# Letting two small stores wait for a row maximum instead of queueing behind the last load

## The chip, the cores and the metric

The kernel runs on one core of a Trainium2 chip. The metric is the device time of one execution in microseconds (us); the medians below are over several executions. SyncE is the engine that issues the transfers here, VectorE and GpSimd compute. A semaphore is a hardware counter that engines raise and wait for.

## The reference

```python
def setup_inputs():
    return {"x": np.random.randn(8192, 8192).astype(np.float32)}

def reference(x):
    return np.linalg.norm(x, ord=np.inf, axis=1)
```

The output is, for each of 8192 rows, the largest absolute value of 8192 float32 numbers: 268 MB are read, 32 KB written.

## The kernel before

SyncE issues all loads on one queue; VectorE takes a maximum over each loaded piece. The first 5888 rows come as 23 loads of 8 MB (two rows per partition). The last 2304 rows (18 per partition) come as 25 loads whose width shrinks to 1280 and 1152 columns, so that little is left to reduce when the last byte has landed (the last maximum reads 1156 columns: 1152 and four partial maxima of its row that lie behind them). Each load signals one of eight semaphores; a load counts as landed when its semaphore has got 16 increments, and the maximum waits for that.

```python
    def load(self, at, w, src):
        ...
        ins = self.nc.sync.dma_start(out=self.ring[:, at : at + w], in_=src)
        ins.then_inc(self.sems[i % SEMS], 16)
        ...
        if i >= SEMS:        # not before the load eight earlier is reduced
            self.tc.add_manual_dep(ins.ins, self.last[i - SEMS].name, ...)
```

The end of the program has three stores. Two of them (23 KB and 8 KB) are ready early; the third holds the last two of the 18 tail rows and needs the last maximum. GpSimd combines the partial maxima of rows that came in pieces, and SyncE waits for the last combination before the third store.

```python
    tc.declare_fence(done.ins, group="loads")
    nc.sync.dma_start(                                            # 128 x 46 floats, 23 KB
        out=out[:split].rearrange("(p q) -> p q", p=P), in_=res_big.rearrange("p t r -> p (t r)")
    )
    out_tail = out[split:].rearrange("(p r) -> p r", p=P)
    nc.sync.dma_start(out=out_tail[:, : ROWS - 2], in_=res_tail[:, : ROWS - 2])   # 8 KB

    seen = nc.sync.keepalive_nop(...)                             # waits for GpSimd
    ...
    last = nc.sync.dma_start(out=out_tail[:, ROWS - 2 :], in_=res_tail[:, ROWS - 2 :])  # 1 KB
```

## Time and profile before

| | before |
|---|---|
| time, median of 3 | 629.49 us |
| the profiled execution itself | 629.77 us, span 627.8 us |
| VectorE busy | 551.9 us (88%) |
| DMA | 428 GB/s over the span |

Read it from the end. Nearly all of the span is one long read, and the question is only what follows the last packet of it: when the last load counts as landed, when the last maximum starts, and when the last store lands. The lines for this are in the prediction.

### The profile page before, as it was taken

What the parts mean: (1) busy time and instruction counts of PE and PEld (TensorE: products, weight loads), DVE (VectorE), ACT (ScalarE), POOL (GpSimd) and SP (SyncE); (2) the same over time, 40 slices, a digit from 0 to 9 for tenths busy, and PEclk for the clock granted to TensorE, in tenths of its full rate; (3) what the DMA queues carried; (4) which work ended last, traced back from release to release, by engine and by line L of the source; (5) the groups of instructions that cost most, each with busy time, mean ns of one, the idle gap of its engine ahead of it and who ended that gap; (6) DMA issues with size and microseconds to landing.
All of it is one profiled execution on the core that took longest, in us unless ns stands there. A gap on an engine that the chain in (4) does not pass through costs nothing.

```text
span 627.8 us, 164 instructions
## 1 busy us (share of the span) xinstructions
DVE 551.9 (88%) x56; POOL 2.9 (0%) x13
## 2 busy tenths in 40 slices
DVE  0588988889988889888898888998889899999998
POOL 0000000000000000000000000000000000000000
DMA  9999999999999999999999999999999999999997
GB/s 401 413 455 409 459 405 463 405 463 401 468 401 468 401 468 401 468 401 468 401 468 401 468 401 468 401 468 401 468 390 435 452 419 438 426 422 431 427 422 284
DMA packets 7344, 268.47 MB, mean 428 GB/s; under 512 B 1200, under 2 KB 1200, under 8 KB 1968
## 3 DMA queue, kind: packets, MB, share of 16 engines
q1 hardware_dynamic: 7344, 268.47, 99.2%
HBM read 268.44 MB, written 0.03 MB: 428 GB/s over the span
## 4 chain that ended last, share of the span: by engine, by line
DMA 59%; DVE 40%; issue 0%; SPq 0%
DMA ring<-in_x_dram 59%; DVE res_big L106 22%; DVE parts L106 10%; DVE res_tail L106 8%; SPq L88 0%
## 5 line engine op out<-in xcount | busy, mean ns | idle before, releaser
L106 DVE TENSOR_REDUCE res_big<-ring 128x2 f32<-128x16384 f32 x23 | 396.1, 17220 | 69.3 <-DMA ring<-in_x_dram 69.3
L106 DVE TENSOR_REDUCE res_tail<-ring 128x1 f32<-128x8192 f32 (+1 forms) x10 | 79.0, 7945 | 2.6 <-DMA ring<-in_x_dram 2.6
L106 DVE TENSOR_REDUCE parts<-ring 128x1 f32<-128x3520 f32 (+17 forms) x19 | 69.8, 3738 | 1.7 <-DMA ring<-in_x_dram 1.7
L106 DVE TENSOR_REDUCE ring<-ring 128x1 f32<-128x1984 f32 (+3 forms) x4 | 7.7, 1982 | 0.0
L202 POOL TENSOR_SCALAR res_tail<-parts 128x1 f32<-128x1 f32 x8 | 2.3, 291 | 614.0 <-DVE parts L106 614.0
L202 POOL TENSOR_SCALAR parts<-parts 128x1 f32<-128x1 f32 x1 | 0.4, 357 | 7.0 <-DVE parts L106 7.0
L237 POOL MEMSET const-bfloat16-1.0<- 128x1 bf16 x1 | 0.1, 103 | 0.0
L237 POOL MEMSET const-uint8-127<- 128x1 uint8 x1 | 0.1, 102 | 0.0
L237 POOL MEMSET const-float32-0.0<- 128x1 f32 x1 | 0.1, 99 | 0.2 <-issue 0.2
L237 POOL MEMSET const-float32-1.0<- 128x1 f32 x1 | 0.1, 99 | 0.0
## 6 DMA issues: line engine op xcount, KB each, us to landing
ring<-in_x_dram SPq DMA_DIRECT2D x3, 4096.0 KB, 41.9
ring<-in_x_dram SPq DMA_DIRECT2D x1, 7488.0 KB, 31.1
ring<-in_x_dram SPq DMA_DIRECT2D x1, 6368.0 KB, 35.4
ring<-in_x_dram SPq DMA_DIRECT2D x1, 5920.0 KB, 40.8
ring<-in_x_dram SPq DMA_DIRECT2D x1, 4800.0 KB, 32.8
ring<-in_x_dram SPq DMA_DIRECT2D x1, 3488.0 KB, 40.4
ring<-in_x_dram SPq DMA_DIRECT2D x1, 3104.0 KB, 39.2
ring<-in_x_dram SPq DMA_DIRECT2D x1, 2944.0 KB, 40.8
```

What stands on the lines that cost most here:

```text
L106: ins = self.nc.vector.tensor_reduce(out=dst, in_=src, axis=mybir.AxisListType.X, op=mybir.AluOpType.max, apply_absolute_value=True,)
L202: combined = nc.gpsimd.tensor_scalar(out=to, in0=best, scalar1=two[0], scalar2=two[1] if len(two) == 2 else None, op0=mybir.AluOpType.max, ...
L237: nc = _bacc.Bacc("TRN2", target_bir_lowering=False, num_devices=1)
```

## The change

The intent is that the two early stores do not stand right behind the last load in the DMA rings, the queues from which the DMA engines take their work. They wait for the last maximum but one (the 1280-column piece), so that they run while VectorE is busy with the last one.

```diff
-    nc.sync.dma_start(
+
+    early = nc.sync.dma_start(
         out=out[:split].rearrange("(p q) -> p q", p=P), in_=res_big.rearrange("p t r -> p (t r)")
     )
     out_tail = out[split:].rearrange("(p r) -> p r", p=P)
-    nc.sync.dma_start(out=out_tail[:, : ROWS - 2], in_=res_tail[:, : ROWS - 2])
+    middle = nc.sync.dma_start(out=out_tail[:, : ROWS - 2], in_=res_tail[:, : ROWS - 2])
+    for store in (early, middle):
+        tc.add_manual_dep(
+            store.ins,
+            pieces.last[-2].name,
+            mybir.DependencyInfo(mybir.DependencyClass.Sync, mybir.DependencyReason.DATA),
+            reason="not beside the last load",
+        )
```

## The prediction

> **What bounds the kernel now.** I read the head of the page first, to see which resource is short over the whole span.
>
> ```profile
> span 627.8 us, 164 instructions
> DVE 551.9 (88%) x56; POOL 2.9 (0%) x13
> DMA  9999999999999999999999999999999999999997
> GB/s 401 413 455 409 459 405 463 405 463 401 468 401 468 401 468 401 468 401 468 401 468 401 468 401 468 401 468 401 468 390 435 452 419 438 426 422 431 427 422 284
> ```
>
> The DMA digits are 9 in every slice but the last. The kernel reads 268.4 MB at 428 GB/s, and 39 of 40 slices cannot change with a diff that touches two stores of 23 and 8 KB near the end. Only the last slice (7 and 284 GB/s) is open. So I asked for the last piece of the chain that ended last, and for the timeline there (columns: start in us, duration in us, engine, line, operation, tiles; in brackets the idle time before it and what ended that).
>
> ```profile
> 609.24 14.89 DMA ring<-in_x_dram
> 624.13 0.02 issue
> 624.15 1.36 DVE res_tail L106
> ```
>
> ```profile
> 622.22 1.48 DVE L106 TENSOR_REDUCE parts<-ring 128x1 f32<-128x1280 f32 x1
> 623.87 0.28 POOL L202 TENSOR_SCALAR res_tail<-parts 128x1 f32<-128x1 f32 x1 [8.68 <-DVE parts L106]
> 624.15 1.36 DVE L106 TENSOR_REDUCE res_tail<-ring 128x1 f32<-128x1156 f32 x1 [0.46 <-DMA ring<-in_x_dram]
> 625.54 0.33 SPq L222 DMA_DIRECT2D out_dram<-res_tail  x1
> ```
>
> The end is a chain: the last load lands at 624.13, the last maximum runs from 624.15 for 1.36 us, the last store is issued at 625.54, and 1.4 us after that it lands. VectorE was free from 622.22 + 1.48 = 623.70 and sat idle for 0.46 us until the load landed. That 0.46 us is the only slack that the change can reach. The DMA view of 609 to 628 us gives each issue's time to landing (count, KB, us):
>
> ```profile
> ring<-in_x_dram SPq DMA_DIRECT2D x1, 576.0 KB, 14.9
> out_dram<-res_big SPq DMA_DIRECT2D x1, 23.0 KB, 14.7
> out_dram<-res_tail SPq DMA_DIRECT2D x1, 8.0 KB, 14.4
> out_dram<-res_tail SPq DMA_DIRECT2D x1, 1.0 KB, 1.4
> ```
>
> The two early stores (23 and 8 KB) are issued at 609.61 and 610.09, right behind the last load (609.24), queue behind eight loads, and land at the same moment as the load whose landing ends the kernel. The last store alone needs 1.4 us.
>
> **Did the stores delay that load?** The answer is in the trace's DMA packets and semaphore increments, which no printed view lists; a load counts as landed at the last of 16 increments. From the first to the last of them the third last load takes 0.43 us (620.09 to 620.51) and the second last 0.44 us (621.67 to 622.11). The last load takes 1.04 us (623.09 to 624.13): nine increments come on time, within 0.31 us, and the other seven trail. Its data were not late. Its last data packet ends at 623.05; the second last load's ends at 621.63, and that load has landed 0.48 us later. The last load needs 1.08 us for the same step. In just that stretch run the stores' packets: 128 of 184 bytes starting from 622.54 to 623.14 and 128 of 64 bytes from 622.64 to 623.22, on engines that had finished their share of the load. Without them I expect the load to land at 623.05 + 0.48 = 623.53. A second way agrees: the second last load (5120 bytes per partition) landed 1.60 us after the one before it; 4608/5120 of that is 1.44, and 622.11 + 1.44 = 623.55.
>
> **What the Trainium skill says.** "DMA: Bandwidth & Descriptors", section "Queues, rings and completion order": on each DMA engine descriptors are taken in ring order, data descriptors carry no barrier, and the semaphore increment is a strongly ordered write that lands only after every earlier write of that engine. Stores queued behind a load can thus overlap its increments; the packets above show the overlap. The page does not say that a later store holds an earlier increment back, so that link is my inference from the 1.04 against 0.44 us. "Perfetto Trace Analysis", section "DMA Instruction — HWDGE (DVE, Sync)": the profiled issue ends when the sequencer is free, and data movement and completion come after it, with a delay that can be surprisingly long when the target is HBM. The trace agrees in kind: the last store's issue is 0.33 us of its 1.42 us to landing, its packets start 0.83 us after the issue began and the last landing comes 0.4 us after the last packet.
>
> **The change, part by part.** Removed: nothing; all three stores and their packets remain. Added: one wait on the DVE semaphore at the first store. The compiled order of instructions on every engine is the same in both kernels, and the second store follows the first in SyncE's order. The loads, the reductions and GpSimd's combinations are untouched. Moved, in steps:
>
> 1. The wait is for the maximum of the 1280-column piece, which ends at 623.70. In this trace SyncE starts about 0.02 us after the increment it waits for, itself some 0.01 us after the instruction's end. So the first store is issued at 623.73 instead of 609.61. It occupies the queue for 0.43 us, then 0.05 us pass (in before 609.61 to 610.09 is 0.48), so the second is issued at 624.21 and SyncE is free at 624.64.
> 2. The last load lands at about 623.54 instead of 624.13: 0.6 us earlier.
> 3. The last maximum cannot use all of it: VectorE is busy to 623.70. It starts at 623.72, after the 0.02 us seen between neighbours. Gain: 624.15 - 623.72 = 0.43 us. It ends at 623.72 + 1.36 = 625.08.
> 4. GpSimd's last combination (623.87 to 624.15) waits on the 1280-column maximum and does not move; it runs beside the last maximum, as earlier ones ran beside theirs without lengthening them (1156 columns with no GpSimd: 1357 ns; 3776 columns with it: 4078 ns; both are 1.04 ns a column plus about 0.15 us).
> 5. The last store needs that combination (624.15), the free queue (624.64) and the last maximum (625.08 + 0.02). The maximum is last by 0.4 us, so the store goes out at 625.10 instead of 625.54 and lands 1.42 us later, at 626.52 instead of 626.96.
> 6. The early stores, given the 1.42 us of the lone store plus 0.1 us for their longer issue, land at about 623.73 + 1.52 = 625.25 and 624.21 + 1.52 = 625.73, both 0.8 us before the last one. The kernel's closing waits then see the last store only.
>
> Sum: -0.43 us, and 629.49 - 0.43 = 629.06 us (span about 627.4).
>
> **The rivals.**
>
> - *The load's late landing is its own.* It is the last in the queue, and perhaps its increments trail because nothing follows it, not because stores do. For it: there is no second load in this trace that ends a queue. Against it: the very last store, with nothing behind it, gets its 16 increments within 0.19 us, and 9 of the load's 16 are on time. Then VectorE still starts at 624.15 and nothing is gained: 629.45 to 629.5.
> - *The stores become the new tail.* If the writes to HBM take over 0.8 us longer than my 1.52 us, the closing wait is for them, or the last store, whose 8-byte pieces lie in the same 72-byte rows as the second store's 64-byte pieces, is held behind them. For it: 256 small packets now enter within 2 us of the end. Against it: in before the same packets took 15 and 11 ns each, 16 of them per engine, or about 0.2 us, and the rings are otherwise empty now. It would eat 0 to 0.8 us: 629.1 to 629.9.
> - *SyncE becomes the bound.* Two issues of 0.48 us fit between 623.73 and 624.69 and the last store wants 625.10. If the issue were delayed by 0.4 us or more, it would push the store one for one. Against: the descriptor work of both was 0.43 us with eight loads in flight, and now the queues are empty. Worth at most a few tenths.
> - *Half the load's delay stays*, for example because it comes from closing traffic in general. VectorE idle would shrink from 0.46 to 0.1 or 0.2 us: about 629.2.
>
> None of these touches more than 2 us of 629: 2% is 12.6 us, and the whole section after the last load's landing is 3.7 us long.
>
> **Range and chances.** The runs of before agree within 0.01 us, so the spread is that of the mechanism. The gain is capped by VectorE at 0.44 us, hence little room below 629.05; I allow 0.15 us there for the closing part to be quicker with fewer things outstanding. Upward I go to no gain at all, 629.50. I give the full gain some 65%, a part of it 15%, none 12%, a loss of some tenths 8%. Within 2%: 99%.
>
> **What would show it.** Right: the last maximum follows its neighbour with no idle time and starts near 623.72; the early stores land in 1.4 to 1.7 us, not 14.7; the last load lands 14.3 us after its issue instead of 14.9, its 16 increments within about 0.45 us; the last store is issued near 625.10 and everything before 609 us is unchanged. Wrong: 0.46 us of idle time still stand before the last maximum (first rival); the early stores land after 626.5, or the last store takes clearly more than 1.42 us (second); the last store is issued well after the last maximum has ended (third). A change of 1 us or more would mean that something before 609 us moved, which this reading excludes.

## The result, and the profile after

The changed kernel took 629.38 us (median of 6, 629.35 to 629.59), the kernel before 629.49 us (median of 6, 629.43 to 629.65). The ratio is 0.9998, 95% interval 0.9986 to 1.0011. A ratio here is the mean time of one kernel's fast runs over that of the other's of the same rounds, so it is not quite the ratio of the medians. The interval includes 1, so these runs alone do not tell the gain from none. The 0.11 us between the medians is a quarter of the 0.43 us foreseen.

The head of the page of the changed kernel (without its GB/s row) is the same but for single tenths:

```profile
span 627.5 us, 164 instructions
DVE 551.8 (88%) x56; POOL 2.8 (0%) x13
DMA  9999999999999999999999999999999999999997
```

Its timeline from 622 us (start in us, duration in us, engine, line, operation, tiles):

```profile
622.47 1.48 DVE L106 TENSOR_REDUCE parts<-ring 128x1 f32<-128x1280 f32 x1
623.86 1.35 DVE L106 TENSOR_REDUCE res_tail<-ring 128x1 f32<-128x1156 f32 x1
623.98 0.35 SPq L213 DMA_DIRECT2D out_dram<-res_big  x1
624.13 0.28 POOL L202 TENSOR_SCALAR res_tail<-parts 128x1 f32<-128x1 f32 x1 [8.69 <-DVE parts L106]
624.37 0.43 SPq L217 DMA_DIRECT2D out_dram<-res_tail  x1
625.24 0.33 SPq L230 DMA_DIRECT2D out_dram<-res_tail  x1
```

There is no bracket with idle time at the last maximum any more. It starts 1.39 us after its neighbour (1.93 before), and the last store is issued 2.77 us after that neighbour's start (625.24 - 622.47; before 625.54 - 622.22 = 3.32). The DMA view from 609 us (KB, us from issue to landing):

```profile
ring<-in_x_dram SPq DMA_DIRECT2D x1, 576.0 KB, 14.3
out_dram<-res_big SPq DMA_DIRECT2D x1, 23.0 KB, 1.5
out_dram<-res_tail SPq DMA_DIRECT2D x1, 8.0 KB, 2.1
out_dram<-res_tail SPq DMA_DIRECT2D x1, 1.0 KB, 1.4
```

The last load lands 0.6 us sooner after its issue, exactly as intended, and its 16 increments spread over 0.57 us like those of the load before it (0.59 us), instead of 1.04 against 0.44.

So the profile shows a larger gain in the tail than the prediction, and the time a much smaller one. Between these two profiled executions the books balance: from the start of the 1280-column maximum to the landing of the last store, 4.75 us before and 4.17 us after, a gain of 0.58; but that maximum started 0.25 us later after the first load's issue (621.75 instead of 621.50), because already the first load landed 0.24 us later (21.98 instead of 21.74 us). The two profiled times differ by 629.77 - 629.44 = 0.33 us, and 0.58 - 0.25 is that. The 0.24 us arose before anything that the change touches. The open question is the 0.58: why do medians not show it?

### The profile page after: what moved, and what is told of

Same layout as the page of the kernel before. It is cut to its first block, busy times and chain, and to the rows that moved or that the text cites. A ratio compares the mean times of both kernels' runs of the same rounds, so it can differ in the third digit from the quotient of the medians.

```text
span 627.5 us, 164 instructions
## 1 busy us (share of the span) xinstructions
DVE 551.8 (88%) x56; POOL 2.8 (0%) x13
## 4 chain that ended last, share of the span: by engine, by line
DMA 57%; DVE 42%; issue 0%; DVEq 0%; SPq 0%
DMA ring<-in_x_dram 57%; DVE res_big L106 22%; DVE parts L106 11%; DVE res_tail L106 8%; DVE ring L106 1%; DVEq L256 0%; SPq L88 0%
```

## The experiments

All kernels gave correct results. The kernels ran on three chips. Two theories:

- **A**: the two stores behind the last load always hold its increments back by about 0.6 us, and the missing gain is lost somewhere else.
- **B**: the size of that delay differs from execution to execution, and the profile before caught a long one.

Times of runs are given with what the traces show: *landing step* is the time from the second last load's landing to the last one's; *idle* is VectorE's idle time before the last maximum; *tail* goes from the start of the 1280-column maximum to the landing of the last store; *first landing* from the first load's issue. *Spread* is the time from the first to the last of a load's 16 increments. Landings are read from the trace's semaphore increments, which no printed view lists.

| kernel (one profile each) | time of that execution, us | landing step | idle | tail | first landing |
|---|---|---|---|---|---|
| before (first profile) | 629.77 | 2.03 | 0.46 | 4.75 | 21.74 |
| before_again | 629.38 | 1.61 | 0.04 | 4.30 | 21.78 |
| before_third | 629.49 | 1.44 | 0 | 4.33 | 21.75 |
| before_fourth | 629.31 | 1.44 | 0 | 4.17 | 21.83 |
| after (first profile) | 629.44 | 1.39 | 0 | 4.17 | 21.98 |
| after_again | 629.24 | 1.38 | 0 | 4.18 | 21.74 |
| after_third | 629.33 | 1.39 | 0 | 4.19 | 21.85 |
| big_behind | 629.66 | 1.40 | 0 | 4.26 | 22.11 |
| small_behind | 629.57 | 1.39 | 0 | 4.18 | 22.09 |
| cut4_behind | 629.72 | 1.76 | 0.20 | 4.45 | 21.94 |
| wait_third | 629.45 | 1.39 | 0 | 4.18 | 21.99 |
| wait_last | 630.21 | 1.40 | 0 | 5.13 | 21.80 |

In the kernels with both stores moved or one left behind, the time of that execution less the first landing is 607.46 to 607.55 us (wait_last apart). In the kernel before it is 608.03, 607.60, 607.74 and 607.48 us. The first landing thus accounts for what the times of undelayed executions differ by: big_behind's 629.66 us is a late start of the stream and no delay at its end. The third profile of before has 0.15 us of its 607.74 in a last store that took 1.54 us to land, instead of 1.4, and the rest before the tail.

### The two kernels again

The three repeats of the kernel before and the two of the changed kernel have no edit.

> The kernel before, once more, for a second profile of its end. The first profile was of an execution of 629.77 us, 0.28 us over the median of 629.49. Theory A (the stores behind the last load always hold its increments back by 0.6 us; the small gain in time comes from elsewhere): spread of the last load's increments near 1.04 us again, VectorE idle 0.4 to 0.5 us before the last maximum, from the start of the 1280-column maximum to the last store's landing 4.75 us. Theory B (the size of that delay differs between executions and the first profile caught a long one): spread of 0.5 to 0.9 us, idle 0 to 0.25 us, 4.2 to 4.6 us to the landing. Time against the kernel before: ratio 1.0000, which shows the noise.

Measured: the last load's increments spread over 0.64 us (those of the load before: 0.45), landing step 1.61 us, idle 0.04 us. Time 629.44 us (629.38 to 629.95, 5 runs). Theory A falls, since it asked for 1.04 us. The same three lines as in the prediction, with 623.78 - (622.26 + 1.48) = 0.04 us of idle time in place of 0.46:

```profile
622.26 1.48 DVE L106 TENSOR_REDUCE parts<-ring 128x1 f32<-128x1280 f32 x1
623.78 1.36 DVE L106 TENSOR_REDUCE res_tail<-ring 128x1 f32<-128x1156 f32 x1
625.16 0.33 SPq L222 DMA_DIRECT2D out_dram<-res_tail  x1
```

> The changed kernel once more. Both theories: no idle time before the last maximum, increments of the last load within the spread of the other loads (0.42 to 0.60 us), 4.1 to 4.25 us from the start of the 1280-column maximum to the last landing. Time: theory A 0.4 to 0.55 us below the kernel before with more runs; theory B 0.05 to 0.25 us below. The load stream's start (21.74 us to the first landing before, 21.98 after) should differ between executions of one kernel, not between kernels.

Measured: landing step 1.38 us, no idle time, tail 4.18 us. Time 629.32 us (629.24 to 629.46, 5 runs) against 629.56 us for the kernel before (9 runs, 629.31 to 629.86), ratio 0.9996, interval 0.9984 to 1.0009. Of the nine runs of before, five lie at 629.31 to 629.56 us and four at 629.82 to 629.86 us. The changed kernel had none in the upper group.

> The kernel before, a third profile. The two so far show the last load landing 2.03 and 1.61 us after the second last, against 1.38 to 1.40 us in the three profiles without the small store behind it, and times that fall into two groups, 629.3 to 629.6 and 629.8 to 629.95 us. Theory B (the stores' delay differs between executions, here 0.2 to 0.65 us): this one lies between 1.55 and 2.1 us and its distance from the first landing to the end of the program explains its time together with the stream's start. If it lies at 1.40 us, the delay is sometimes absent.

Measured: landing step 1.44 us and no idle time, so the delay is 0.05 us over the 1.39 us of the changed kernel: outside the range that I gave, in the direction of "sometimes absent". Time 629.45 us (629.23 to 629.50).

> The kernel before, a fourth profile. The last load landed 2.03, 1.61 and 1.44 us after the second last in the first three, against 1.38 to 1.40 us in every profile without both stores behind it. Expected: again between 1.40 and 2.1 us, a different size; idle time before the last maximum is this number less 1.57 us, where positive. Time 629.2 to 629.9 us.

Measured: landing step 1.44 us, as in the third, so not a new size as expected; idle none; time 629.45 us (629.31 to 629.80). Its timeline stands for the quiet kind of execution of the kernel before:

```profile
622.33 1.48 DVE L106 TENSOR_REDUCE parts<-ring 128x1 f32<-128x1280 f32 x1
623.72 1.35 DVE L106 TENSOR_REDUCE res_tail<-ring 128x1 f32<-128x1156 f32 x1
625.10 0.33 SPq L222 DMA_DIRECT2D out_dram<-res_tail  x1
```

From 622.33 to 625.10 is 2.77 us, what the changed kernel needs. In this execution there was nothing to gain.

> The changed kernel, a third profile. Expected: 1.37 to 1.41 us between the last two landings, no idle time, 4.15 to 4.25 us from the start of the 1280-column maximum to the last landing; no execution over 629.65 us. With the runs of the kernel before pooled, a mean gain of 0.1 to 0.25 us.

Measured: landing step 1.39 us, tail 4.19 us, time 629.37 us (629.30 to 629.54), before in the same rounds 629.34 us (629.14 to 629.74), ratio 1.0000, interval 0.9987 to 1.0013. On this chip the medians show no gain at all. Pooled, the kernel before has 48 timed runs (mean 629.49, 11 of them above the changed kernel's highest by 0.05 us or more) and the changed kernel 16 (mean 629.39, none above 629.59). The difference of 0.11 us has a standard error of 0.04 us, taken as if the runs were independent; one of the four groups had no runs of the changed kernel, and without it the difference is 0.14 us. By group it is 0.10, 0.27 and 0.05 us between the means. No group's own ratio is clear of 1.

### One store moved, the other left

```diff
-    for store in (early, middle):
+    for store in (middle,):          # big_behind: the 23 KB store stays behind the last load
```

> Only the 8 KB store waits; the 23 KB store stays behind the last load. If it is the stores' packets in the rings that hold the last load's increments back and the large one is enough: spread 0.8 to 1.04 us and idle 0.2 to 0.46 us, as before, time as before. If each store adds its half: spread 0.7 to 0.8 us, idle 0.1 to 0.2 us. If the delay is only the last load's own (rival of the prediction, which the profile after speaks against): no difference to before.

Measured: landing step 1.40 us, idle none, spread of the last load's increments 0.78 us against 0.79 for the load before it, so there is no delay, neither the whole nor the half that I expected. Time 629.47 us (629.43 to 629.66). The 8 KB store, alone now, lands quickly:

```profile
out_dram<-res_big SPq DMA_DIRECT2D x1, 23.0 KB, 14.0
out_dram<-res_tail SPq DMA_DIRECT2D x1, 8.0 KB, 1.4
```

The 2.1 us that it took in the changed kernel's profile come with going right behind the 23 KB store; the other kernels that send it there show 1.7 to 2.1 us.

```diff
+    middle = nc.sync.dma_start(out=out_tail[:, : ROWS - 2], ...)   # small_behind: first, no wait
     early = nc.sync.dma_start(out=out[:split]..., in_=res_big...)
-    for store in (early, middle):
+    for store in (early,):
```

> The counterpart of big_behind, where the 23 KB store alone behind the last load did not delay it (1.40 us after the second last, no idle time): here the 8 KB store alone stays behind the last load and the 23 KB store waits. If one store alone does no harm and it takes both: 1.38 to 1.45 us, no idle time before the last maximum, time 629.3 to 629.5. If the 8 KB store is the culprit: 1.6 to 2.0 us, idle time 0.04 to 0.46 us. In both cases the 23 KB store, issued after the second last maximum, lands in 1.4 to 1.7 us, before the last store.

Measured: landing step 1.39 us, no idle time; time 629.32 us (629.20 to 629.57). Neither store alone delayed the load in its one profile. As the pair also failed to do so in two of four, these two profiles do not prove that it takes both.

### More packets behind the load

```diff
-    nc.sync.dma_start(out=out[:split]..., in_=res_big...)
+    for c in range(0, 48, 12):
+        e = min(c + 12, 2 * n_big)
+        nc.sync.dma_start(out=out_big[:, c:e], in_=all_big[:, c:e])
```

> The kernel before, with the 23 KB store cut into four stores behind the last load: 640 instead of 256 store packets in the rings. If the store packets hold the last load's increments back, the spread grows to 1.3 to 2.5 us and the time by 0.3 to 1.5 us over the kernel before. If the delay does not depend on how much stands behind the load: spread as before (1.04 or less), time within 0.1 us of before, since SyncE's four issues end (611.5 us) long before the load lands.

Measured: spread 0.94 us against 0.60 for the load before, landing step 1.76 us, idle 0.20 us; time 629.45 us (629.36 to 629.72), as before. The delay is there, 0.37 us over the quiet 1.39, but it has not grown with 2.5 times the packets: it is no longer than what the pair alone has shown. The 1.3 us or more that a fixed cost per packet asked for did not come, in this one profile of a delay that differs between executions.

### Other maxima to wait for

```diff
-            pieces.last[-2].name,
+            pieces.last[-1].name,    # wait_last
```

> Both early stores wait for the very last maximum instead of the last but one. The last load is as free as in the changed kernel (1.39 us after the second last), but SyncE now issues three stores in a row after the last maximum: 0.35 + 0.04 + 0.43 + 0.05 = 0.87 us before the last one. Expected: from the start of the 1280-column maximum to the last landing 4.17 + 0.85 = 5.0 us or more, time 0.6 to 1.1 us over the changed kernel and 0.5 to 0.9 us over the kernel before. If SyncE's issue did not matter here, 4.2 us and no loss.

Measured: 630.43 us (630.21 to 630.59) against 629.50 us, ratio 1.0016, interval 1.0002 to 1.0030. The timeline:

```profile
623.67 1.34 DVE L106 TENSOR_REDUCE res_tail<-ring 128x1 f32<-128x1156 f32 x1
625.04 0.35 SPq L213 DMA_DIRECT2D out_dram<-res_big  x1
625.44 0.43 SPq L217 DMA_DIRECT2D out_dram<-res_tail  x1
625.91 0.43 SPq L230 DMA_DIRECT2D out_dram<-res_tail  x1
```

The last store goes out 625.91 - 625.04 = 0.87 us late, as worked out, and takes 0.1 us more to land. The 0.93 us over the kernel before are just above the 0.5 to 0.9 expected. SyncE's time to issue stores is therefore a real cost as soon as nothing covers it. In the changed kernel the last maximum covers it: its second early store ends at 624.37 + 0.43 = 624.80, and the last store needs the queue at 625.24.

```diff
-            pieces.last[-2].name,
+            pieces.last[-3].name,    # wait_third
```

> The early stores wait for the last maximum but two, 1.4 us earlier than in the changed kernel. By that kernel's profile the 23 KB store is issued about 621.9 us after the first load's issue, its packets start near 622.7, right when the last load's data packets have ended (622.6) and before its increments are in (623.1); the 8 KB store's packets come near 623.2, after them. If only packets that are already queued behind the load, both kinds, delay it: 1.38 to 1.41 us between the last two landings, as in the changed kernel, same time. If any small write to HBM in the 0.45 us between last data and last increment delays it: 1.5 to 2.0 us, idle time up to 0.4 us, time 0.1 to 0.4 us over the changed kernel.

Measured: landing step 1.39 us, no idle time, time 629.45 us (629.33 to 629.54; the changed kernel 629.37 us in the same rounds). The 23 KB store's packets ran from 622.70 to 622.93 us after the first issue, between the last load's last data packet (622.57) and its last increment (623.00), and did no harm. That is one profile, of one store in that window.

### Samples in the middle of the stream

One profile of the end gives one sample of the delay. Two kernels put extra stores of zeros, into a spare tensor in HBM, behind many loads of the main stream.

```diff
+    KINDS = ("none", "both", "large", "small", "apart", "onchip")   # N = 30 loads
+    # probes_two: ("none", "both", "none", "apart"), N = 24
+        if kind in ("both", "large"):    # 184 bytes per partition, side by side
+            nc.sync.dma_start(out=to[: P * 46].rearrange("(p q) -> p q", p=P), in_=extra[:, :46])
+        if kind in ("both", "small"):    # 64 bytes per partition in rows of 72 bytes
+            rows = to[P * 128 : P * 146].rearrange("(p q) -> p q", p=P)
+            nc.sync.dma_start(out=rows[:, :16], in_=extra[:, 46:])
+        if kind == "apart":              # the same two, in rows of 1024 bytes
+            rows = to.rearrange("(p q) -> p q", p=P)
+            nc.sync.dma_start(out=rows[:, :46], in_=extra[:, :46])
+            nc.sync.dma_start(out=rows[:, 128:144], in_=extra[:, 46:])
+        if kind == "onchip": ...         # the same two, from SBUF to SBUF
...
         pieces.load(at, R * n_cols, x_big[t])
+        probe(t)
```

> The changed kernel with extra stores of zeros behind the first 30 loads, in rotation: none, a pair of 23 and 8 KB as in the kernel before, the 23 KB one alone, the 8 KB one alone, the pair into rows 1 KB apart, and the pair copied within SBUF. Five samples of each, to see what delays the increments of the load in front. If writes to HBM in the pair do it whatever the place: spread of the load's increments 0.1 to 0.6 us over that of loads with none for the pair and the pair apart, none for the copy within SBUF. If sharing of neighbouring lines does it: not for the pair apart. If anything in the rings does it: for all. If it takes the end of the queue (nothing behind the stores): for none.

> As the first probes, with only none, the pair into neighbouring places, none, and the pair into rows 1 KB apart, behind the first 24 loads, six samples of each. If what holds the increments back is that the stores' pieces are neighbours in HBM: the mean offset of the increments from the first one is 0.05 to 0.3 us larger for loads with the neighbouring pair than for the quiet load after them, in all six, and within 0.03 us for the pair apart. If five samples of the first probes misled: both the same.

The measure is how far, on average, a load's 16 increments lie behind its first one. An engine that has fallen behind for good shifts this for all later loads, so each is compared with a quiet neighbour. The first probes' expectation spoke of the spread; I went over to this mean after seeing them, and the second probes' expectation was written in it beforehand. In us:

```
first probes, both minus the "none" load just before it:     0.07 0.13 0.07 0.18 0.26
first probes, both minus the "apart" load three loads later:  0.04 0.02 0.07 0.12 0.17
first probes, apart minus the "onchip" load just after it:   0.01 -0.01 -0.02 -0.01 0.00
second probes, both minus the "none" load just after it:     0.05 0.13 0.10 0.12 0.14 0.15
second probes, apart minus the load just after it:           0.00 0.02 0.01 0.03 0.01 0.00
```

Eleven of eleven loads with the neighbouring pair behind them have later increments than their quiet neighbour, by 0.05 us or more, and none of eleven with the pair apart is over 0.03 us. In the first row a lasting lag of an engine that begins at that load counts too; the second row, against a later load, leaves it out, and there one of five is under 0.03 us. The effect is on some engines only: the 13th load of the second probes (counted from 0) has its increments at 0.00 to 0.39 us for ten engines, at 0.85 to 0.90 for five, and at 1.23 for the last; those of the quiet load after it are at 0.46, 0.47, 0.56, 0.57, 0.78 and 0.93 for the same six places. In the first probes the large store alone gave on average 0.04 us more than the spread-out pair two loads later, and the small one alone 0.01 us more than the spread-out pair one load later, on average less than the pair together (0.08 us in the second row). But one of the five loads with the large store alone, the 8th counted from 0, had its last increment at 1.41 us, where the next four loads have theirs at 0.98 to 1.03: that one store alone never delays an increment is not shown. The copy within SBUF, with as many packets in the same rings, adds nothing beyond 0.04 us against the load after it.

So packets in the rings are not enough to delay the load in front, and neither are small writes to HBM as such: with the same two sizes of piece it depended on how the pieces lie in HBM, close together and unaligned or spread out. Which of the two it is, close or unaligned, these runs do not separate: the spread-out rows are also aligned. The probes also cost time of their own: 633.08 us and 632.00 us for one run each, and single engines stayed behind to the end (spread of the increments 0.61 us at the first load of the second probes, 0.95 us at the 30th).

## Why the prediction was right or wrong, point by point

The time lies in the predicted range and within 2%, but that was easily had: the range reached up to no gain at all, and 2% is 12.6 us. The size of the gain is not right: 0.11 us instead of 0.43 us.

**Step 1, the issue of the stores.** Right. It foresaw the first store 1.51 us after the start of the 1280-column maximum (623.73 - 622.22); the profile after has 623.98 - 622.47 = 1.51. The store occupied the queue for 0.35 instead of 0.43 us.

**Step 2, the last load lands 0.6 us earlier.** This is the term that was mis-sized. The mechanism is right: with both stores out of its way the landing step was 1.38 to 1.39 us in all three profiles (1.42 to 1.44 foreseen), and a pair of stores can make the increments in front of it late, as the probes show. But the kernel before shows the delay as 0.64, 0.22, 0.05 and 0.05 us over 1.39 in four profiles. I took the first as a constant of the kernel, although its own execution was 0.28 us slower than the median, which was the sign that it was not typical. The sum mixed two executions: it took a gain read from one of 629.77 us off a median of 629.49 us. Taken off its own time, 0.43 us gives 629.34 us, which is near the 629.38 us measured. That the three runs of before agreed within 0.01 us was luck: the 48 runs lie between 629.14 and 629.95 us. A detail of the recorded text is loose, too: by its own lines the two stores landed not with the load (624.13) but at 609.61 + 14.7 = 624.31 and 610.09 + 14.4 = 624.49.

**Step 3, VectorE takes 0.43 us of it.** VectorE's idle time was 0.46, 0.04, 0 and 0 us. What the change gains up to the issue of the last store is, from the four profiles of before, 3.33, 2.90, 2.79 and 2.77 us against 2.76 to 2.77 us after: 0.56, 0.13, 0.02 and 0.00, on average 0.18 us. The pooled times say 0.11 with an error of 0.04. Where the full delay occurs the gain is even larger than foreseen, because the last maximum does not start 0.02 us after its neighbour's end but 0.09 us before it (623.86 against 622.47 + 1.48 = 623.95). The Trainium skill, "Perfetto Trace Analysis", section "DVE / Act Engine Instruction (TENSOR_ADD, Activation, etc)", would have told me: the recorded end includes the acknowledgement of the writes, and the next instruction may begin its prefetch before that. The trace agrees: neighbours overlap by 0.07 to 0.09 us in all profiles without idle time. I had taken the 0.02 us from a start that waited for a DMA; the first profile of before already had overlaps of 0.09 us between the maxima before it.

**Step 4, GpSimd.** Right: its combination starts 1.66 us after the 1280-column maximum (1.65 foreseen) and does not hold anything up.

**Step 5, the last store waits for the last maximum.** Right in order. Issue 2.77 us after the 1280-column maximum's start where 2.88 was foreseen, by the overlap just named, and 1.39 us to landing where 1.42 was.

**Step 6, the early stores land 0.8 us before the last.** Half right. The 23 KB store took 1.47 us (1.52 foreseen) and landed 1.2 us before the last store, as the step's own times say (626.52 - 625.25 = 1.27, not 0.8). The 8 KB store took 2.1 us, not 1.52, and landed only 0.17 us before the last store. The second rival, stores as the new tail, was nearer than I gave it credit for, but did not come about: the closing wait is still for the last store.

**The rivals.** The first, that the last load is late by itself, is refuted by the changed kernel's profiles. The third, SyncE as the bound, did not occur, and the experiment that waits for the last maximum shows that it would have cost 0.87 us. The fourth, half the delay staying, did not occur either; instead the delay was mostly absent before the change. I had no rival that said so, and that is the one that happened.

**What stays open.** Why the pair sometimes delays the last load by 0.64 us and sometimes by 0.05, although its packets started at nearly the same time after the first load's issue in all four profiles of before (the first at 621.82 to 621.92 us); whether one store alone can do it at the end of the stream; how a later write in a ring holds up an earlier increment. And the times of before with an upper group (629.65 to 629.95, 11 of 48 runs): that they are executions with a long delay fits the one profile of before that lies there (629.77), but a late start of the stream can give such a time as well (629.66 in big_behind), and the other timed runs have no trace.

## What to carry to other kernels

Small stores that are ready early can make a load in front of them land late, so behind a load whose landing ends the kernel they are better held back: let them wait for an event near that landing which still leaves other work to cover the queue's time to issue them (0.4 us each here). Expect tenths of a microsecond at most, as here, and in some executions nothing. Before the size of a delay in one profile goes into a sum, compare the profiled execution's own time with the median, and take a second profile. Where a delay comes in some executions only, look at the upper end of the times as well: none of 16 runs of the changed kernel lies above 629.59 us, against 12 of 48 before, while mean and median both moved by 0.1 us. That the slow ones among those runs are the ones with a long delay is not shown.

## What the Trainium skill lacked or had wrong

- "DMA: Bandwidth & Descriptors", section "Queues, rings and completion order": it says that an increment lands after every earlier write of its engine, and nothing on later ones. Here small writes to HBM that follow in the ring made a load's increments late: by 0.05 to 0.64 us at the end of the stream (four profiles), by 0.05 to 0.26 us on average over the engines in eleven samples within it (0.02 to 0.17 us for the first five of them by the stricter measure), and by at most 0.03 us where the pieces lay in rows of 1 KB.
- The same page, section "Latency and other measured facts", and "Perfetto Trace Analysis", section "DMA Instruction — HWDGE (DVE, Sync)", tell of long completion of writes to HBM without a figure for one small store right behind another: 8 KB landed in 1.4 us alone and in 1.7 to 2.1 us right behind a 23 KB store.
- No page says how much one kernel's executions differ in the DMA stream itself: here the first 8 MB load landed 21.74 to 21.98 us after its issue in three profiles of the changed kernel and 21.74 to 22.11 us in all twelve, whose loads are the same, with the spread of its 16 increments between 0.44 and 0.89 us.
